# A hybrid attention block in float32 on one core: latent queries in six packed column tiles, one rope for all heads

## The chip, the cores and the metric

The kernel runs on one core of one Trainium2 chip. The metric is the device time of one execution in microseconds (us); less is better. The engines are PE (matrix multiply; PEld is its weight load), DVE (vector), ACT (scalar), POOL (GpSimd), and SP, whose queue issues nearly all DMAs here.

## The reference

One decoder layer on x of 1024 rows by 1024 columns: two parallel token mixers, gates, and a gated feed-forward block. The change touches the second mixer, multi-head latent attention (MLA), with 8 heads:

```python
cq = rmsnorm(q_lat, q_norm_g[l])                       # 1024 x 384
qb = (cq @ w_uq[l]).reshape(B, S, MLA_HEADS, MLA_QK_DIM)   # 96 = 64 + 32 per head
q_nope, q_rope = jnp.split(qb, [MLA_NOPE_DIM], axis=-1)
q_rope = apply_rope(q_rope, cos_b, sin_b)
ckv = rmsnorm(kv_lat, kv_norm_g[l])                    # 1024 x 256
kvb = (ckv @ w_ukv[l]).reshape(B, S, MLA_HEADS, MLA_NOPE_DIM + MLA_V_DIM)
k_nope, vb = jnp.split(kvb, [MLA_NOPE_DIM], axis=-1)
k_rope = apply_rope(k_r[:, :, None, :], cos_b, sin_b)[:, :, 0, :]   # one for all heads
o_b = mla_attention(q_nope, q_rope, k_nope, k_rope, vb)
```

`mla_attention` is causal softmax attention in query blocks of 128. `apply_rope` turns the two 16-wide halves x1, x2 of the 32 rope columns into x1 cos - x2 sin and x2 cos + x1 sin.

## The kernel before

Every float32 product is made of three matmuls on a high and a low part of each operand (`mm3`, lines 167 to 169), so each operand is first split: a copy on ACT (`split`, line 160) and a subtraction on DVE or POOL (line 161). The program runs in stages: input projections, sliding-window attention with the gate products woven in (`gate_step`, one product of 12 matmuls of 512 columns each), the MLA, the output projections, and the feed-forward block. In the MLA stage each engine's order of instructions is set by a scheduler at build time, from the order of the code; at run time each engine works strictly in that order, and a DMA on SP's queue waits there until its buffer or its data is ready, with all later ones behind it.

The MLA has two parts. The **front** (328 to 368 us of the trace) turns the latents round (`latent_T`, tiles lT), runs the last six gate products (tiles fa and fb; their results go are stored to memory by SP), and makes the first queries, keys and all values. Its matmul results share a pool of four PSUM buffers (`P1`) with most other tiles. Then a **loop of 64 steps**, 8 heads of 8 query blocks, follows. A step t emits the scores of step t+2 (`scores`, three matmuls for each stretch of keys), the value product of an earlier step (`pv`, tiles ob), a query or key product for a later head if one is due, and the transposes of its own probabilities (`transposes`, tiles pTb, then p split into pth and ptl). Between the scores and the transposes of a step lie a maximum on DVE (line 1148), an exponential on ACT (1149) and a division on POOL (1150, 1151).

Queries before: `prod_q(h, s)` makes, for one head h and one half s of the 1024 rows, 128 result rows in 9 matmuls of 512 columns: 64 plain rows, 32 rope rows and the same 32 with the halves swapped, from weights that hold these columns twice. One DVE product with a table (`rope_t`, tile qf) applies cosine, sine and scale; ACT and POOL split the result into qT. The scores then contract over all 128 rows, against keys whose 32 rope rows stand twice. There are 16 such tiles: two ahead of the loop, the others in steps 2 and 4 of heads 0 to 6. `prod_k(j, s)` makes the keys of two heads in 6 matmuls; each result is split for two heads, 64 rows apiece. `prod_v(b)` makes the values of one block of 128 rows for all heads in 6 matmuls; all eight stand ahead of the first scores.

## Time and profile before

| | |
|---|---|
| device time, median of three runs (range) | 1362.41 us (1362.39 to 1362.61) |
| span of the profiled execution, its own time from first to last instruction | 1359.5 us |
| PE busy | 1339.6 us, 99% of the span |
| share of PE in the chain of work that ended last | 88% |
| MLA front | 328.0 to 368.3 us |
| MLA loop, heads 0 to 6 | 368.3 to 517.9 us |

The profile is of one execution. A busy engine is not an engine at its peak: matmuls overlap, so one that is listed with 0.39 us is followed by the next after 0.23 us. A wait is named by what ended it. A window is a stretch of the span, given by its start and end; here they are the front, head 0 and heads 1 to 6 of the loop, each head from its first scores to those of the next. [...]

### The profile page before, as it was taken

What the parts mean: (1) busy time and instruction counts of PE and PEld (TensorE: products, weight loads), DVE (VectorE), ACT (ScalarE), POOL (GpSimd) and SP (SyncE); (2) the same over time, 40 slices, a digit from 0 to 9 for tenths busy, and PEclk for the clock granted to TensorE, in tenths of its full rate; (3) what the DMA queues carried; (4) which work ended last, traced back from release to release, by engine and by line L of the source; (5) the groups of instructions that cost most, each with busy time, mean ns of one, the idle gap of its engine ahead of it and who ended that gap; (6) DMA issues with size and microseconds to landing.
All of it is one profiled execution on the core that took longest, in us unless ns stands there. A gap on an engine that the chain in (4) does not pass through costs nothing.

```text
span 1359.5 us, 18989 instructions
## 1 busy us (share of the span) xinstructions
PE 1339.6 (99%) x6600; PEld 1120.0 (82%) x6600; DVE 912.7 (67%) x1495; ACT 642.8 (47%) x1299; POOL 557.7 (41%) x610
## 2 busy tenths in 40 slices
PE   9999999999999999999999999999999999999997
PEld 6899878878788888888887888888888888888886
DVE  7868767676777887585448866666656654664862
ACT  7434766675577776652336322323232332644453
POOL 2116645553166554200031465766665551022521
PEclk9999999999999999999999999999999999999999
DMA  9455322335100110671243353644434425996504
GB/s 366 154 189 163 119 86 82 113 117 182 51 2 13 44 47 17 241 239 63 105 174 132 119 181 139 235 178 169 152 144 171 170 83 183 375 382 246 170 9 147
DMA packets 78096, 202.25 MB, mean 149 GB/s; under 512 B 8753, under 2 KB 15409, under 8 KB 78001
## 3 DMA queue, kind: packets, MB, share of 16 engines
q1 hardware_dynamic: 77856, 201.04, 41.5%
q8 instruction: 52, 0.85, 0.3%
q14 instruction: 44, 0.35, 0.1%
q10 hardware_dynamic: 144, 0.00, 0.0%
HBM read 141.24 MB, written 59.77 MB: 148 GB/s over the span
## 4 chain that ended last, share of the span: by engine, by line
PE 88%; DVE 4%; issue 3%; POOL 2%; ACT 2%; DMA 0%; SPq 0%; POOLq 0%; ACTq 0%; DVEq 0%
PE fa L169 7%; PE fa L167 7%; PE fa L168 7%; PE fb L169 6%; PE fb L167 6%; PE fb L168 6%; PE fd L167 5%; PE fd L169 5%; PE fd L168 5%; PE pTb L1165 2%; PE xo L169 2%; PE xo L167 2%; PE xo L168 2%; PE ob L1188 1%; PE oA L167 1%
## 5 line engine op out<-in xcount | busy, mean ns | idle before, releaser
L161 DVE TENSOR_TENSOR wl<-wr,wl 128x512 fp32r<-128x512 f32 x150 | 153.6, 1048 | 72.2 <-ACT wl L160 71.9
L161 DVE TENSOR_TENSOR lrv<-lr,lrv 128x1024 fp32r<-128x1024 f32 x77 | 105.2, 1397 | 49.9 <-ACT lrv L160 48.8
L160 ACT CAST lrv<-lr 128x1024 fp32r<-128x1024 f32 x77 | 80.3, 1054 | 96.0 <-PE fd L169 56.0
L167 PE MATMUL fd<-lrv 128*128 128x512 f32 x308 | 119.8, 389 | 0.0
L168 PE MATMUL fd<-lrv 128*128 128x512 f32 x308 | 119.8, 389 | 0.0
L169 PE MATMUL fd<-lrv 128*128 128x512 f32 x308 | 119.8, 389 | 0.0
L172 POOL TENSOR_TENSOR wr<-wr,sm 128x512 f32<-128x512 f32 (+1 forms) x38 | 46.4, 1229 | 149.1 <-DVE wl L161 116.4
L160 ACT CAST wl<-wr 128x512 fp32r<-128x512 f32 x150 | 87.0, 624 | 2.4 <-DVE wr L820 2.2
L299 POOL TENSOR_SCALAR ms<-ss 128x1 f32<-128x1 f32 x32 | 8.8, 274 | 189.1 <-ACT xn L1534 111.7
L161 DVE TENSOR_TENSOR wl<-sm,wl 128x512 fp32r<-128x512 f32 x60 | 47.5, 818 | 45.1 <-ACT wl L160 45.0
L169 PEld LDWEIGHTS fd<-lrv 128*128 128x128 f32 x308 | 57.8, 188 | 12.1
L168 PEld LDWEIGHTS fd<-lrv 128*128 128x128 f32 x308 | 57.8, 188 | 12.1
L167 PEld LDWEIGHTS fd<-lrv 128*128 128x128 f32 x308 | 57.8, 188 | 11.8
L1150 POOL TENSOR_TENSOR denb<-denb,neg_one 128x1 f32<-128x1 f32 x64 | 36.5, 571 | 74.4 <-ACT p L1149 64.7
L1149 ACT ACTIVATE p<-scb,nmb 128x384 f32<-128x384 f32 (+3 forms) x64 | 47.6, 745 | 35.9 <-DVE nmb L1148 34.1
L161 DVE TENSOR_TENSOR ptl<-pTb,pth 128x512 fp32r<-128x512 f32 (+2 forms) x96 | 50.1, 550 | 13.8 <-ACT pth L160 13.0
L1148 DVE CUSTOM_DVE_ANT_0 scb<-scb,mask 128x384 f32<-128x384 f32 (+3 forms) x64 | 48.6, 759 | 14.0 <-PE scb L1140 13.7
L1426 ACT ACTIVATE act<-sm 128x512 f32<-128x512 f32 x11 | 7.0, 636 | 104.8 <-DVE sm L175 104.8
L1151 POOL TENSOR_SCALAR p<-p,denb 128x384 f32<-128x384 f32 (+3 forms) x64 | 49.8, 778 | 6.3
L160 ACT CAST pth<-pTb 128x512 fp32r<-128x512 f32 (+2 forms) x96 | 43.0, 483 | 13.6 <-PE pTb L1165 13.1
L167 PE MATMUL fb<-t2h,wl 128*128 128x512 f32 x120 | 47.4, 395 | 0.0
L167 PE MATMUL fb<-t3h,wl 128*128 128x512 f32 x120 | 47.3, 394 | 0.0
(346 smaller groups left out, 4287.3 us busy)
## 6 DMA issues: line engine op xcount, KB each, us to landing
lr<-la_d SPq DMA_DIRECT2D x77, 256.0 KB, 5.4
wr<-in_w_gate_dram SPq DMA_DIRECT2D x22, 512.0 KB, 3.8
wr<-in_w_up_dram SPq DMA_DIRECT2D x22, 512.0 KB, 5.0
wd<-in_w_down_dram SPq DMA_DIRECT2D x22, 512.0 KB, 6.8
rb_d<-wd SPq DMA_DIRECT2D x22, 512.0 KB, 2.6
la_d<-sd SPq DMA_DIRECT2D x22, 512.0 KB, 5.4
lr<-rb_d SPq DMA_DIRECT2D x44, 256.0 KB, 5.4
lr<-in_w_down_dram SPq DMA_DIRECT2D x33, 256.0 KB, 5.6
```

What stands on the lines that cost most here:

```text
L160: nc.scalar.copy(hi, src)
L161: (eng or nc.vector).tensor_tensor(lo, src, hi.bitcast(F32), op=ALU.subtract)
L167: nc.tensor.matmul(ps, ah, bh, start=first and i == 0, stop=False, skip_group_check=go_on)
L168: nc.tensor.matmul(ps, ah, bl, start=False, stop=False, skip_group_check=go_on)
L169: nc.tensor.matmul(ps, al, bh, start=False, stop=last and i == n - 1, skip_group_check=go_on)
L172: eng.tensor_tensor(out, a, b, op=ALU.subtract)
L1148: nc.vector.tensor_tensor_reduce(s_, s_, m_, 1.0, -NEG, op0=ALU.add, op1=ALU.min, accum_out=nm)
L1149: nc.scalar.activation(p_, s_, AF.Exp, scale=-1.0, bias=nm, accum_out=den)
L1150: nc.gpsimd.tensor_tensor(den, den, neg_one[:, 0:1], op=ALU.pow)
L1151: nc.gpsimd.tensor_scalar(p[:, 0:w], p[:, 0:w], den, 0.0, op0=ALU.mult, op1=ALU.add)
L1165: nc.tensor.transpose(pp[:, i], p[:, blk(k0 + i)], ident)
L1188: nc.tensor.matmul(po[:, q_off:], vst, lo[:, kb % 4, q_off:], start=False, stop=kb == nk - 1)
```

## The change

The query weights are packed anew in six column tiles of 128: two rope tiles (the first, and the second, 16 rope columns of all 8 heads) and four plain tiles (64 columns of two heads each). `prod_rope(s)` runs in the front: two tiles of 9 matmuls for half s, four DVE products with cosine and sine tables, a subtraction and an addition on POOL, a split on ACT and POOL, and two stores to a scratch tensor rq_d. `prod_q(j, s)` now makes two heads in 9 matmuls, splits the plain rows from PSUM for each head on ACT and DVE (`activation`, then `scalar_tensor_tensor`), and fetches each head's 32 rope rows from rq_d into rows 64 to 95 of its qT tile by two DMAs. So 12 tiles of 9 matmuls stand where 16 stood. Keys hold their rope rows once; they are split into one key tile and copied into the two others by DMA. The scores contract over 96 rows. One product `prod_q` and one `prod_k` remain ahead of the first scores, the second halves of both follow in the code, and the eight `prod_v` stand two each in steps 0 to 3. Later query products fall in step 4 of heads 0, 2, 4 and step 2 of heads 1, 3, 5. Weight units of queries are three, not four; the mask is made on POOL; loads and splits of the oa tiles stand at other steps.

```diff
+    def prod_rope(s):
+        cos, sin = (r[:, half(s)] for r in rope_cs)
+        r1, r2 = (U("rr", F32, (P, 2, 512)) for _ in range(2))
+        for i, w in enumerate(wrope):
+            ps = P1("r")
+            mm3(ps, [((w[:, 0, k], w[:, 1, k]), (cq[k][0][:, half(s)], cq[k][1][:, half(s)])) for k in range(3)])
+            nc.vector.tensor_tensor(r1[:, i], ps, sin if i else cos, op=ALU.mult)
+            nc.vector.tensor_tensor(r2[:, i], ps, cos if i else sin, op=ALU.mult)
+        sub(r1[:, 0], r1[:, 0], r1[:, 1], nc.gpsimd)
+        add(r1[:, 1], r2[:, 0], r2[:, 1], nc.gpsimd)
+        t = V("rq", F32R, (P, 2, 2, 512))
+        split(t[:, 0], t[:, 1], r1, nc.gpsimd)
+        for i in range(2):
+            nc.sync.dma_start(rq_d[i][:, :, half(s)], t[:, :, i].bitcast(F32))
...
+    for t in k_tiles:
+        if kT:
+            nc.sync.dma_start(t[64:QK].bitcast(F32), k_tiles[0][64:QK].bitcast(F32))
+        kT.append((t[:, 0], t[:, 1]))
...
+    def load_rope(h, s):
+        for i in range(2):
+            r = 64 + 16 * i
+            nc.sync.dma_start(rope_rows[h][r:r + 16, :, half(s)].bitcast(F32), rq_d[i][16 * h:16 * h + 16, :, half(s)])
+
+    def prod_q(j, s):
...
+        for h in (2 * j, 2 * j + 1):
+            load_rope(h, s)
+        w = wuq[j // 2][j % 2]
+        ps = P1("q")
+        mm3(ps, [((w[:, 0, k], w[:, 1, k]), (cq[k][0][:, half(s)], cq[k][1][:, half(s)])) for k in range(3)])
+        for u in range(2):
+            hi, lo = (t[0:64, half(s)] for t in qT[2 * j + u])
+            src = ps[64 * u:64 * u + 64]
+            nc.scalar.activation(hi, src, AF.Copy, scale=-SC_B)
+            nc.vector.scalar_tensor_tensor(lo, src, -SC_B, hi.bitcast(F32), op0=ALU.mult, op1=ALU.subtract)
...
-    def prod_q(h, s):
-        if s == 0:
-            qT[h] = hi_lo("qT")
-        w = wuq[h // 2][h % 2]
-        ps = P1("q")
-        mm3(ps, [((w[:, 0, k], w[:, 1, k]), (cq[k][0][:, half(s)], cq[k][1][:, half(s)])) for k in range(3)])
-        qf = U("qf")
-        nc.vector.tensor_tensor(qf[:, 0:512], ps, rope_t[:, half(s)], op=ALU.mult)
-        split(qT[h][0][:, half(s)], qT[h][1][:, half(s)], qf[:, 0:512], nc.gpsimd)
...
-            nc.tensor.matmul(sc[:, o], qh[:, blk(n)], kh[:, kc], start=True, stop=False)
+            nc.tensor.matmul(sc[:, o], qh[0:QK, blk(n)], kh[0:QK, kc], start=True, stop=False)
...
-    prod_k(0, 0)
-    prod_k(0, 1)
-    for b in range(NB):
-        prod_v(b)
...
+        if t < 4:
+            for b in (2 * t, 2 * t + 1):
+                prod_v(b)
...
-            if n in (2, 4):
-                prod_q(h + 1, n // 2 - 1)
+        nj = h // 2 + 1
+        if 2 * nj < NH:
+            if (h % 2, n) == (0, 4):
+                prod_q(nj, 0)
+            if (h % 2, n) == (1, 2):
+                prod_q(nj, 1)
```

PE where the first scores stand. Before (v: a value product, scb: scores):

```order
L167 MATMUL v_4155<-wv_3970,ckv_3854 128x512
L168 MATMUL v_4155<-wv_3970,ckv_3854 128x512
L169 MATMUL v_4155<-wv_3970,ckv_3854 128x512
L1138 MATMUL scb_4168<-kT_3994,qT_4037 128x384
L1139 MATMUL scb_4168<-kT_3994,qT_4037 128x384
L1140 MATMUL scb_4168<-kT_3994,qT_4037 128x384
L1138 MATMUL scb_4179<-kT_3994,qT_4037 128x512
L1139 MATMUL scb_4179<-kT_3994,qT_4037 128x512
L1140 MATMUL scb_4179<-kT_3994,qT_4037 128x512
```

And now:

```order
L168 MATMUL v_4200<-wv_4058,ckv_3936 128x512
L169 MATMUL v_4200<-wv_4058,ckv_3936 128x512
L167 MATMUL v_4210<-wv_4058,ckv_3935 128x512
L168 MATMUL v_4210<-wv_4058,ckv_3935 128x512
L1168 MATMUL scb_4135<-kT_4001,qT_4078 128x384
L1169 MATMUL scb_4135<-kT_4001,qT_4078 128x384
L1170 MATMUL scb_4135<-kT_4001,qT_4078 128x384
L1168 MATMUL scb_4164<-kT_4001,qT_4078 128x512
L1169 MATMUL scb_4164<-kT_4001,qT_4078 128x512
L1170 MATMUL scb_4164<-kT_4001,qT_4078 128x512
L169 MATMUL v_4210<-wv_4058,ckv_3935 128x512
L167 MATMUL v_4210<-wv_4058,ckv_3936 128x512
```

The first scores stand inside the second value product, where all eight stood ahead of them.

ACT in the front, ahead of the key tiles (cq and ckv: latents turned round; wl and sm: gate weights; wuq: query weights; rq: the roped rows; krT: the keys' rope rows). Before:

```order
L160 CAST wl_3919<-wr_3565 128x512
L160 CAST wl_3950<-wr_3565 128x512
L160 CAST ckv_3853<-lT_3936 128x512
L160 CAST ckv_3854<-lT_3943 128x512
L160 CAST wv_3970<-wr_3895 128x512
L160 CAST wv_3969<-wr_3895 128x512
L160 CAST wv_3970<-wr_3897 128x512
L160 CAST wv_3969<-wr_3897 128x512
L160 CAST kT_3994<-krT_3997 64x512
L160 CAST kT_3994<-krT_4008 64x512
```

And now:

```order
L160 CAST rq_3913<-rr_3885 128x1024
L160 CAST wl_3918<-sm_3676 128x512
L160 CAST ckv_3935<-lT_3937 128x512
L828 COPY go_3933<-fa_3778 128x512
L160 CAST ckv_3936<-lT_3944 128x512
L160 CAST wl_3984<-wr_3558 128x512
L160 CAST wuq_4034<-wr_3815 128x384
L160 CAST wuq_4037<-wr_3815 128x384
L160 CAST wl_4040<-wr_3558 128x512
L160 CAST rq_3979<-rr_3951 128x1024
L160 CAST kT_4001<-krT_4004 32x512
L160 CAST kT_4001<-krT_4011 32x512
```

Two casts of rq stand in the row, each of which needs POOL's sum; the second stands ahead of the casts that empty the two krT tiles.

SP's queue in the front (go: gate results, rq: rows to the scratch tensor, qT: rope rows out of it). Before:

```order
L840 DMA gate_d<-go_3891 128x512
L1058 DMA rope_t_3967<-c_rope_t_dram 128x1024
L840 DMA gate_d<-go_3891 128x512
L840 DMA gate_d<-go_3991 128x512
L1070 DMA gate_d<-go_3991 128x512
L254 DMA wr_4204<-in_w_uq_dram 128x768
```

And now:

```order
L1065 DMA rq_d<-rq_3913 256x1x512 x2
L838 DMA gate_d<-go_3933 128x512
L1065 DMA rq_d<-rq_3979 256x1x512 x2
L1084 DMA kT_4002<-kT_4001 32x2048
L1084 DMA kT_4003<-kT_4001 32x2048
L838 DMA gate_d<-go_3933 128x512
L1097 DMA qT_4078<-rq_d 16x2x512 x2
L1097 DMA qT_4079<-rq_d 16x2x512 x2
L838 DMA gate_d<-go_4075 128x512
L1122 DMA gate_d<-go_4075 128x512
L1097 DMA qT_4078<-rq_d 16x2x512 x2
L1097 DMA qT_4079<-rq_d 16x2x512 x2
```

The rope rows of the second half for heads 0 and 1 (last two rows) are issued behind the last gate store (line 1122), which stood last before too (line 1070).

## Rows read from the trace of the kernel before

**Rows 1.** page, part 1 (busy time) and part 4 (chain that ended last).
```profile
PE 1339.6 (99%) x6600; PEld 1120.0 (82%) x6600; DVE 912.7 (67%) x1495; ACT 642.8 (47%) x1299; POOL 557.7 (41%) x610
...
PE 88%; DVE 4%; issue 3%; POOL 2%; ACT 2%; DMA 0%; SPq 0%; POOLq 0%; ACTq 0%; DVEq 0%
```

**Rows 2.** windows: length, busy PE, PEld, DVE, ACT, POOL (instructions); clock, DMA, GB/s.
```profile
328.00:368.33 40.33, 40.16 (x199) 32.70 (x198) 29.61 (x48) 22.43 (x41) 2.53 (x2) 1.00 0.36 128
368.33:384.50 16.17, 15.03 (x89) 12.48 (x87) 10.92 (x25) 10.18 (x24) 10.18 (x15) 1.00 0.00 1
384.50:407.20 22.70, 22.70 (x146) 19.76 (x143) 17.71 (x38) 16.15 (x38) 14.00 (x19) 1.00 0.01 2
407.20:427.20 20.00, 19.98 (x133) 17.49 (x131) 14.66 (x32) 14.29 (x34) 12.61 (x18) 1.00 0.06 20
427.20:450.70 23.50, 22.71 (x146) 19.79 (x144) 18.47 (x38) 16.20 (x38) 13.58 (x19) 1.00 0.08 23
450.70:471.20 20.50, 20.14 (x132) 17.53 (x131) 16.67 (x34) 15.87 (x37) 11.75 (x17) 1.00 0.15 46
471.20:495.00 23.80, 22.79 (x146) 19.76 (x144) 19.69 (x42) 17.35 (x40) 14.17 (x21) 1.00 0.14 40
495.00:517.90 22.90, 21.86 (x145) 18.98 (x143) 19.97 (x38) 18.36 (x41) 12.23 (x17) 1.00 0.10 30
```

**Rows 3.** timeline of PE: start, us, instruction [idle before <- releaser].
```profile
346.67 1.04 PE L1065 MATMUL krT<-ident,lat 128*64 128x128 f32 x8
347.46 0.47 PE L167 MATMUL fa<-hh,wl 128*128 128x512 f32 x1
...
357.45 0.39 PE L167 MATMUL v<-wv,ckv 128*128 128x512 f32 x1
...
368.33 0.33 PE L1138 MATMUL scb<-kT,qT 128*128 128x384 f32 x1
...
370.50 0.50 PE L1138 MATMUL scb<-kT,qT 128*128 128x512 f32 x1 [0.78 <-ACT p L1149]
...
378.36 1.09 PE L1165 MATMUL pTb<-ident,p 128*128 128x128 f32 x8 [0.33 <-POOL p L1151]
```

**Rows 4.** timeline of PE: sliding-window scores, half of them with 64 rows.
```profile
203.80 1.23 PE L901 MATMUL sc<-khd,qs 128*128 128x256 f32 x7 [0.17 <-DVE qs L887]
204.86 0.40 PE L167 MATMUL fb<-t3h,wl 128*128 128x512 f32 x1
```

**Rows 5.** waits of PE, 340 to 545 us: total, times, longest.
```profile
PE pTb L1165 <- POOL p L1151: 1.9, 4, 0.7
PE scb L1138 <- ACT p L1149: 1.5, 2, 0.8
PE k L167 <- DVE ob L1199: 1.5, 2, 0.8
PE q L167 <- DVE ptl L161: 0.7, 2, 0.3
```

**Rows 6.** groups by tile: count, ns min/median/max, first and last start.
```profile
L1088 DVE TENSOR_TENSOR qf<-q,rope_t x16: 673/692/692, 354.0 to 518.3; 128x512 f32<-128x512 f32 x16
L161 DVE TENSOR_TENSOR kT<-k,kT x16: 677/688/694, 356.9 to 498.9; 64x512 fp32r<-64x512 f32 x16
L160 ACT CAST kT<-k x16: 567/583/586, 356.3 to 498.3; 64x512 fp32r<-64x512 f32 x16
L161 DVE TENSOR_TENSOR wl<-wr,wl x150: 674/694/1785, 128.1 to 1132.0; 128x512 fp32r<-128x512 f32 x150
L161 POOL TENSOR_TENSOR qT<-qf,qT x16: 1271/1292/1723, 355.4 to 519.7; 128x512 fp32r<-128x512 f32 x16
```

**Rows 7.** DMA issues, 300 to 560 us: KB each, us to landing.
```profile
gate_d<-go SPq DMA_DIRECT2D x9, 256.0 KB, 2.2
oa_d<-oa SPq DMA_DIRECT2D x1, 512.0 KB, 3.1
```

**Rows 8.** timeline of SP's queue: start, us, issue.
```profile
352.53 0.32 SPq L1070 DMA_DIRECT2D gate_d<-go  x1
```

More of the change, by code (lines that the diff above doesn't have):

```diff
@@ L202, in hybrid_block_kernel @@
     lat_d = dram.tile([NB, P, LAT], F32, name="lat_d")
+    rq_d = dram.tile([2, P, 2, S], F32, name="rq_d")
     gate_d = dram.tile([16, P, S], F32, name="gate_d")
@@ L287, in hybrid_block_kernel @@
         ukv_unit(k)
-    for j in range(1, 4):
-        uq_unit(j)
+    uq_unit(2)
     for nm, dp in (("oa", 0), ("oa", 1), ("oa", 2), ("ob", 0), ("ob", 1), ("oa", 3), ("ob", 2), ("ob", 3)):
@@ L1038, in latent_T @@
         split(dst[0][:, half(s)], dst[1][:, half(s)], pt.rearrange("p b c -> p (b c)"))
-    load_lat(NB)
+    rope_cs = [U("rope_cs") for _ in range(2)]
+    for t in range(2):
+        nc.sync.dma_start(rope_cs[t], c_rope_t[t])
+    wrope = st.get(("uq", 0))
+    st.load_to(st.index[("ukv", 1)])
     cq = [hi_lo("cq") for _ in range(3)]
@@ L1044, in hybrid_block_kernel @@
     gate_step()
-    ckv = [hi_lo("ckv") for _ in range(2)]
     for j in range(3):
         latent_T(j * P, cq[j], 1)
+    def prod_rope(s):
[12 more added lines that the diff above has]
+            nc.sync.dma_start(rq_d[i][:, :, half(s)], t[:, :, i].bitcast(F32))
@@ L1048, in hybrid_block_kernel @@
+    prod_rope(0)
     gate_step()
-    st.load_to(st.index[("ukv", 1)])
+    ckv = [hi_lo("ckv") for _ in range(2)]
     for j in range(2):
         latent_T(C_CKV + j * P, ckv[j], 0)
-    st.conv_to(st.index[("uq", 0)])
+    prod_rope(1)
     gate_step()
+    kT = []
+    k_tiles = [V("kT", F32R, (P, 2, S)) for _ in range(3)]
+    for s in range(2):
+        pr = P1("krT", (ROPE_B, 4, P))
+        for j in range(4):
+            nc.tensor.transpose(pr[:, j], lat[4 * s + j][:, C_RT:C_CKV], ident)
+        t = k_tiles[0][64:QK]
+        split(t[:, 0, half(s)], t[:, 1, half(s)], pr.rearrange("p b c -> p (b c)"))
@@ L1054, in hybrid_block_kernel @@
+    for t in k_tiles:
+        if kT:
+            nc.sync.dma_start(t[64:QK].bitcast(F32), k_tiles[0][64:QK].bitcast(F32))
+        kT.append((t[:, 0], t[:, 1]))
     for j in range(2):
         latent_T(C_CKV + j * P, ckv[j], 1)
+    wuq = {0: st.get(("uq", 1))}
     gate_step()
-    rope_t = U("rope_t")
-    nc.sync.dma_start(rope_t, c_rope_t)
-    st.conv_to(st.index[("ukv", 1)])
-    gate_step()
-    kT = [hi_lo("kT") for _ in range(3)]
-    for s in range(2):
-        pr = P1("krT", (HD, 4, P))
-        for j in range(4):
-            nc.tensor.transpose(pr[:, j], lat[4 * s + j][:, C_RT:C_CKV], ident)
-        for hi, lo in kT:
-            split(hi[64:128, half(s)], lo[64:128, half(s)], pr.rearrange("p b c -> p (b c)"))
+    qT = {}
@@ L1731, in _constants @@
     c, s = tables(ROPE_B)
-    rt = np.concatenate([np.ones((64, S), np.float32), c.T, c.T, -s.T, s.T]).astype(np.float32) * np.float32(-SC_B)
+    rt = np.stack([np.tile(t.T, (NH, 1)) for t in (c, s)]) * np.float32(-SC_B)
     q = np.arange(P)[:, None]
```

60 lines of the change are left out of this document (34 added, 26 removed).

## The prediction

> **What bounds the kernel now.** I read the busy times and the chain of waits first: PE is busy 99% of the span and holds 88% of the chain that ended last [rows 1]. So a matmul less is worth its price, as long as PE stays the last to be ready. Whether it does is read by stretch. In the windows PE has 40.16 of 40.33 us in the front, 15.03 of 16.17 in head 0, and in heads 1 to 6 between 20.00 and 23.80 us a head with 0.0, 0.0, 0.8, 0.4, 1.0 and 1.0 us idle [rows 2]. The reader is to see the second column there: DVE has 17.7, 14.7, 18.5, 16.7, 19.7 and 20.0 us of work in these heads, 73% to 87% of their length. PE bounds each head, with DVE some 13% behind it in head 6. The waits name what PE stops for: probabilities from POOL (1.9 us), a score buffer that ACT has to empty (1.5 us), and PSUM buffers for k and q that DVE empties late (1.5 and 0.7 us) [rows 5].
>
> **Price of a matmul.** From the first value matmul at 357.45 us to the first score at 368.33 us lie the 48 of the values: 10.88 / 48 = 0.2267 us each for 512 columns [rows 3]. Eight transposes take 347.46 - 346.67 = 0.79 us, 0.1 us each [rows 3].
>
> **The change part by part.**
>
> *Query tiles.* Before 16 x 9 = 144 matmuls, after 12 x 9 = 108: 36 x 0.2267 = 8.2 us less for PE. It is not spread evenly. Up to the end of head 0 PE now does the four rope tiles (36), three plain tiles (27), the keys (12) and the values (48): 123, where 18 + 18 + 12 + 48 = 96 stood. That is 27 x 0.2267 = **6.1 us more** there. In heads 1 to 6 twelve query tiles become five: 63 x 0.2267 = **14.3 us less**, 2.04 us in each of heads 1 to 5 and 4.08 us in head 6. So all of the gain, and the loss ahead of it, hangs on whether these six heads get shorter.
>
> *Scores over 96 rows.* No gain: seven score matmuls of 256 columns, half of them over 64 rows, take 204.86 - 203.80 = 1.06 us, 0.15 each [rows 4], which is not under the 0.11 that 256 columns cost at 0.2267 per 512. I count 0.
>
> *Values in the first steps.* Their 48 matmuls stay. Now PE idles 0.78 and 0.33 us after the first scores, waiting for ACT and POOL with nothing left to do [rows 3]; in the new order value matmuls stand between the first scores and the first transposes. I take **-1.1 us** (bounds 0 and -1.1). Their eight casts and splits go with them: two of 0.6 and 0.7 us a step on ACT and DVE, while PE gains 12 x 0.2267 = 2.7 us a step, which covers them.
>
> *The rope in the front.* It adds eight DVE products (0.69 each, by qf), on POOL four operations of 1.29 us and two of twice the columns, estimated at 2.6 us, and two ACT casts of 1024 columns, estimated at 1.2 us from 0.58 for 512 [rows 6]. It takes out two qf, four of the six key splits, and the mask on DVE. POOL has 2.53 us of work in the 40 us of the front, and DVE 29.61, so there is room [rows 2]. What can show on PE is a wait: ACT's second cast of rq waits for POOL's sums, and behind it stand the casts that empty the krT tiles, whose PSUM buffer the next gate product needs. From the last rope matmul: one DVE product 0.7, two POOL sums 2.6, the cast 1.2, the key cast 0.6, its DVE split 0.7, together 5.7 us. PE has 14 gate matmuls and 16 transposes in the meantime, 3.2 + 1.6 = 4.8 us. The rest is **+1.0 us**. Bounds: 0 (the buffer is free earlier) and 5: a weight split on DVE (wl) takes 0.694 us in the median and 1.785 at worst [rows 6], and if ten such splits of the front are each 1.1 us late because POOL is now at work, PE may wait for about half of these 11 us, DVE having 10.7 us free there. I take the 1.0, since the median wl shows nothing of it.
>
> [...]
>
> *DMAs.* New on SP's queue: four stores of 512 KB to rq_d, two key copies, 32 loads of rope rows (64 KB each). The nearest landings are 2.2 us for 256 KB and 3.1 for 512 KB [rows 7]. The last to be needed early are the second-half rope rows of heads 0 and 1, wanted by the third set of scores. They stand behind the last gate store. That was issued at 352.53 us [rows 8]; with 36 rope and 9 query matmuls now ahead of that gate product (10.2 us) and the wait of 1.0 it goes at about 363.7, four loads at 0.3 to 0.4 us behind it end at 365.3, and they land at about 368. The first scores stand at 368.33 - 0.9 (74 matmuls ahead of them, not 78) + 1.0 = 368.4, and between the first two sets and the third stand 24 value matmuls, 5.4 us: needed at about 375. Seven us of slack, so **0**.
>
> *The six heads.* PE's work falls to 20.7, 17.9, 20.7, 18.1, 20.8 and 17.8 us. DVE's hardly falls: two splits of 0.69 a tile (by kT, same rows and columns) where two qf stood [rows 6]; only in head 6 it loses a qf, 19.3 us left. POOL loses 14 x 1.29 us. If no head runs with DVE over 87% busy, the highest share now, the heads take 20.7, 17.9, 21.2, 19.2, 22.6 and 22.2 = 123.8 us against 133.4: they give back 9.6. If idle time stays as it is they give back 14.3. I take the middle, **-12.0 us**: DVE may well go past 87%, with POOL's splits gone and two of six query-weight splits left in the loop, but each query tile now holds its PSUM buffer for four operations (0.58 + 0.69, twice) instead of one of 0.69.
>
> **Sum.** +6.1 - 1.1 + 1.0 + 0 - 12.0 = -6.0 us. The profiled span of 1359.5 would become 1353.5; the median of the runs lies 2.9 us over that span, so **1356.4 us**.
>
> **Rivals.**
>
> *PE keeps the bound everywhere.* No wait in the front and heads 1 to 6 without idle: they give back 14.3, up to 14.3 + 3.2 with their present idle gone. 6.1 - 1.1 - 14.3 = -9.3, down to -12.5: 1349.9 to 1353.1 us. For it: PE is busy 95% to 100% of each head [rows 2]. Against: the waits that PE has are for DVE, ACT and POOL [rows 5], and they come nearer with less work between them. Chance 0.20.
>
> [...] Heads 1 to 6 give back 3.3 to 8.7: the time stays within 2.7 us, 0.2%, about what a measurement of this kernel can tell from no change: 1359.7 to 1365.1. For it: DVE at 87% in head 6, with 1.0 us of PE idle there already. Against: heads 1 and 2 have DVE at 78% and 73% and no idle at all. Chance 0.16.
>
> *Slower: the heads keep their pace.* If the path from scores through DVE, ACT and POOL to the transposes set the pace of a step, the 6.1 us ahead would stay and the heads would give back under 3.3: over 1365.1, up to 1362.4 + 6.0 = 1368.4. It decides where a head gives back less than a quarter of its 2.04. Against: a head with keys takes about 3 us more than one without (23.50 to 20.00), which is what its 12 matmuls cost (2.7), so PE sets the pace. Chance 0.07. Late rope rows would do the same, but need 7 + 6.0 + 2.7 = 16 us beyond the landings shown: 0.02.
>
> **How the numbers follow.** The forecast, 1353.1 to 1359.7 us, gets the rest, 0.55. It and the first rival are faster by over 0.2%: 0.75; same 0.16; slower 0.09. The range of 8 in 10 takes the forecast, most of the first rival and the lower part of the second: 1351.0 to 1361.5.
>
> **What would show it.** Right: the first scores within 1.5 us of 368.4; head 1 begins about 6 us later than now (384.5), at 389 to 391; heads 1 to 5 each 1 to 2 us shorter and head 6 some 2 us shorter, with more PE idle in head 6 than 1.0; no wait of PE on a DMA; a wait of about 1 us of a gate product after the krT transposes. Wrong: PE waiting for krT's or wl's DVE operations by several us in the front, or heads that keep 20 to 24 us with PE idle in them, or scores that wait for qT's loads.

## The result, and the profile after

The changed kernel takes 1365.95 us (median of 14 runs, 1363.69 to 1367.54), against 1362.40 for the kernel before in the same session (14 runs). The ratio is 1.0024, with a 95% interval of 1.0016 to 1.0032: slower by about 3.5 us, where 6.0 less were forecast, and above the range. The profiled spans say the same, 1359.5 before and 1363.5 after, so the steps of the prediction can be checked in one pair of traces.

The page of the changed kernel, parts 1 and 4, against [rows 1]:

```profile
PE 1336.9 (98%) x6564; PEld 1115.7 (82%) x6564; DVE 911.6 (67%) x1487; ACT 640.2 (47%) x1295; POOL 545.7 (40%) x602
...
PE 84%; DVE 4%; issue 4%; POOL 3%; ACT 2%; DMA 1%; SPq 0%; POOLq 0%; ACTq 0%; DVEq 0%
```

PE's busy time fell by only 2.7 us where 8.2 us of matmuls were taken out: a part of the rest is matmuls at a granted clock of 0.50, shown below. Its share of the chain fell by four points: waits have come in. The windows of the changed kernel show where (columns as in [rows 2]: length, busy PE, PEld, DVE, ACT, POOL, then the granted clock). The first row is the front (with 1.7 us ahead of its first transposes, which stand at 327.69 us here and at 328.00 before), then head 0, then heads 1 to 6, then two short stretches:

```profile
326.00:371.28 45.28, 42.83 (x203) 34.52 (x202) 30.77 (x46) 20.40 (x37) 12.64 (x10) 0.96 0.56 183
371.28:395.90 24.62, 22.00 (x120) 18.30 (x118) 15.60 (x31) 13.70 (x31) 8.91 (x14) 1.00 0.08 24
395.90:417.20 21.30, 20.98 (x136) 17.95 (x133) 17.55 (x38) 15.34 (x35) 8.94 (x14) 1.00 0.06 16
417.20:437.30 20.10, 18.80 (x121) 16.01 (x122) 15.77 (x33) 14.87 (x36) 11.54 (x18) 1.00 0.04 11
437.30:458.70 21.40, 20.79 (x137) 18.04 (x135) 17.50 (x38) 15.33 (x36) 9.40 (x16) 1.00 0.09 29
458.70:478.30 19.60, 18.68 (x121) 15.93 (x122) 15.56 (x33) 15.10 (x36) 11.12 (x18) 1.00 0.04 11
478.30:500.20 21.90, 21.29 (x139) 18.33 (x137) 18.19 (x39) 16.24 (x37) 9.48 (x15) 1.00 0.21 62
500.20:522.40 22.20, 18.34 (x125) 15.97 (x125) 19.91 (x41) 19.45 (x45) 10.83 (x16) 1.00 0.14 48
353.80:357.10 3.30, 3.30 (x9) 2.62 (x8) 3.04 (x6) 3.25 (x7) 2.77 (x2) 0.50 0.02 5
524.50:527.70 3.20, 3.10 (x11) 2.18 (x10) 2.29 (x6) 1.97 (x5) 2.70 (x4) 0.50 0.02 5
```

Three things are to be seen. The first scores stand at 371.3 instead of 368.3 us, and head 1 begins at 395.9 instead of 384.5: 11.4 us later, where about 6 were forecast. Heads 1 to 6 take 126.5 us instead of 133.4: 6.9 less, where 12.0 were forecast. And in two stretches the granted clock is 0.50, where it was 1.00 in each window of the MLA before [rows 2].

PE's waits between 340 and 545 us (total, times, longest), against [rows 5]:

```profile
PE pTb L1195 <- POOL p L1181: 6.5, 10, 1.4
PE scb L1168 <- ACT p L1179: 2.8, 4, 1.8
PE fb L167 <- DVE sm L175: 1.4, 1, 1.4
PE lT L1037 <- DVE rr L1059: 0.5, 1, 0.5
PE r L167 <- ACT go L828: 0.5, 1, 0.5
```

The waits for k and q of before (2.2 us) are gone; those for probabilities grew from 1.9 to 6.5 us, those for a score buffer from 1.5 to 2.8, and three in the front are new, 2.45 us together. What made the front wait is read from the timelines of DVE, POOL and ACT side by side (start, us, instruction):

```profile
344.68 2.40 DVE L161 TENSOR_TENSOR wl<-sm,wl 128x512 fp32r<-128x512 f32 x1 [3.14 <-ACT wl L160]
...
349.40 0.68 DVE L1058 TENSOR_TENSOR rr<-r,rope_cs 128x512 f32<-128x512 f32 x1
350.00 0.68 DVE L1059 TENSOR_TENSOR rr<-r,rope_cs 128x512 f32<-128x512 f32 x1
350.59 1.44 DVE L161 TENSOR_TENSOR wl<-wr,wl 128x512 fp32r<-128x512 f32 x1
351.96 0.68 DVE L175 TENSOR_TENSOR sm<-fb,pu 128x512 f32<-128x512 f32 x1
```

```profile
344.14 2.39 POOL L161 TENSOR_TENSOR rq<-rr,rq 128x1024 fp32r<-128x1024 f32 x1 [1.16 <-ACT rq L160]
350.22 1.27 POOL L172 TENSOR_TENSOR rr<-rr 128x512 f32<-128x512 f32 x1 [3.68 <-DVE rr L1058]
351.56 1.61 POOL L175 TENSOR_TENSOR rr<-rr 128x512 f32<-128x512 f32 x1
```

```profile
343.01 1.05 ACT L160 CAST rq<-rr 128x1024 fp32r<-128x1024 f32 x1 [7.68 <-POOL rr L175]
343.97 0.61 ACT L160 CAST wl<-sm 128x512 fp32r<-128x512 f32 x1
344.49 0.58 ACT L160 CAST ckv<-lT 128x512 fp32r<-128x512 f32 x1
344.96 0.59 ACT L828 COPY go<-fa 128x512 f32<-128x512 f32 x1
```

DVE's weight split at 344.68 is listed with 2.40 us where its kind takes 0.69; it ends at 347.08, half a microsecond after POOL's split (346.53). The one at 350.59 ends half a microsecond after POOL's subtraction. All that stands behind them on DVE is late: the products that free PE's rope tiles, and the gate addition sm at 351.96, for which PE then waits. But DVE was late before that. Ahead of the split at 344.68 it had stood idle for 3.14 us until ACT cast the same weights, and this cast stood on ACT behind the first cast of rq, which waited for POOL's sums. So did the copy of go, which ends the first of PE's three waits (0.51 us, at 345.60). The other two:

```profile
350.73 0.66 PE L1037 MATMUL lT<-ident,lat 128*128 128x128 f32 x4 [0.54 <-DVE rr L1059]
352.78 0.47 PE L167 MATMUL fb<-t4h,wl 128*128 128x512 f32 x1 [1.40 <-DVE sm L175]
353.09 0.40 PE L168 MATMUL fb<-t4l,wl 128*128 128x512 f32 x1
...
354.26 0.63 PE L169 MATMUL fb<-t4h,wl 128*128 128x512 f32 x1
354.69 0.63 PE L167 MATMUL fb<-t4h,wl 128*128 128x512 f32 x1
```

About a microsecond behind the second of them the granted clock falls to 0.50 (353.8 to 357.1 us). Matmuls start 0.43 us apart instead of 0.227; over the 3.3 us of the row above that loses about 3.3 x (1 - 0.227 / 0.43) = 1.6 us. At 524.5 us the same happens (0.50 to 527.7) behind waits of 1.82 and 0.74 us.

### The profile page after: what moved, and what is told of

Same layout as the page of the kernel before. It is cut to its first block, busy times and chain, and to the rows that moved or that the text cites. A ratio compares the mean times of both kernels' runs of the same rounds, so it can differ in the third digit from the quotient of the medians.

```text
span 1363.5 us, 18998 instructions
## 1 busy us (share of the span) xinstructions
PE 1336.9 (98%) x6564; PEld 1115.7 (82%) x6564; DVE 911.6 (67%) x1487; ACT 640.2 (47%) x1295; POOL 545.7 (40%) x602
## 4 chain that ended last, share of the span: by engine, by line
PE 84%; DVE 4%; issue 4%; POOL 3%; ACT 2%; DMA 1%; SPq 0%; POOLq 0%; ACTq 0%; DVEq 0%
PE fa L169 7%; PE fa L167 7%; PE fa L168 7%; PE fb L169 6%; PE fb L167 6%; PE fb L168 6%; PE fd L167 5%; PE fd L169 5%; PE fd L168 5%; PE xo L167 2%; PE xo L169 2%; PE xo L168 2%; PE pTb L1195 1%; PE oA L167 1%; PE oA L169 1%
## 5 line engine op out<-in xcount | busy, mean ns | idle before, releaser
L168 PE MATMUL fd<-lrv 128*128 128x512 f32 x308 | 119.8, 389 | 0.0
L167 PE MATMUL fd<-lrv 128*128 128x512 f32 x308 | 119.8, 389 | 0.0
L1178 DVE CUSTOM_DVE_ANT_0 scb<-scb,mask 128x384 f32<-128x384 f32 (+3 forms) x64 | 48.5, 760 | 13.6 <-PE scb L1170 12.5
L1195 PE MATMUL pTb<-ident,p 128*128 128x128 f32 x288 | 45.8, 280 | 7.2 <-POOL p L1181 6.5
L167 PE MATMUL fb<-t4h,wl 128*128 128x512 f32 x120 | 47.8, 398 | 1.4 <-DVE sm L175 1.4
```

Source lines behind the costliest of these rows:

```text
L167: nc.tensor.matmul(ps, ah, bh, start=first and i == 0, stop=False, skip_group_check=go_on)
L168: nc.tensor.matmul(ps, ah, bl, start=False, stop=False, skip_group_check=go_on)
L1178: nc.vector.tensor_tensor_reduce(s_, s_, m_, 1.0, -NEG, op0=ALU.add, op1=ALU.min, accum_out=nm)
L1195: nc.tensor.transpose(pp[:, i], p[:, blk(k0 + i)], ident)
```

## The experiments

All times of a row are from its own profile, except the median and the ratio to the kernel before (with its 95% interval), which are from the timed runs; the kernel before was timed again beside each group of runs, so the ratios are to be compared, not the medians. Where a row leaves a part of the work out, its text says so.

| kernel | median us | ratio to before | span us | first scores | head 1 begins | heads 1 to 6, us |
|---|---|---|---|---|---|---|
| before | 1362.4 | 1 | 1359.5 | 368.3 | 384.5 | 133.4 |
| changed | 1365.95 | 1.0024 (1.0016 to 1.0032) | 1363.5 | 371.3 | 395.9 | 126.5 |
| e2 rope sums on DVE | 1367.38 | 1.0033 (1.0021 to 1.0046) | 1365.6 | 371.2 | 397.4 | 127.2 |
| e8 rope sums left out | 1359.61 | 0.9974 (0.9965 to 0.9984) | 1358.1 | 364.8 | 389.2 | 126.5 |
| e10 sums on DVE, late | 1362.27 | 1.0003 (0.9994 to 1.0012) | 1359.8 | 367.5 | 392.1 | 126.6 |
| e3 values ahead | 1365.98 | 1.0028 (1.0018 to 1.0039) | 1363.5 | 380.2 | 395.9 | 126.6 |
| e4 rope rows early | 1364.54 | 1.0015 (1.0006 to 1.0024) | 1361.5 | 371.1 | 394.6 | 126.5 |
| e1 before, fewer q | 1356.33 | 0.9956 (0.9943 to 0.9968) | 1354.6 | 369.8 | 386.0 | 126.1 |
| e16 changed, fewer q | 1363.14 | 1.0004 (0.9995 to 1.0013) | 1361.7 | 371.4 | 396.1 | 124.7 |
| e14 no low part of p | 1358.68 | 0.9967 (0.9956 to 0.9979) | 1354.8 | 370.2 | 394.8 | 119.8 |
| e15 no scaling of p | 1358.90 | 0.9974 (0.9964 to 0.9984) | 1355.9 | 370.4 | 393.3 | 122.7 |
| e9 reciprocal on DVE | 1363.00 | 1.0010 (1.0001 to 1.0018) | 1362.8 | 372.0 | 396.1 | 124.9 |
| e13 same, in before | 1361.55 | 0.9992 (0.9984 to 1.0001) | 1360.2 | 369.2 | 385.1 | 132.1 |
| e5 keys spread | 1365.22 | 1.0020 (1.0011 to 1.0029) | 1362.4 | 368.2 | 393.9 | 127.4 |
| e6 splits earlier | 1364.85 | 1.0013 (1.0004 to 1.0022) | 1363.1 | 371.4 | 396.0 | 127.6 |
| e7 e4, e5, e6 joined | 1364.67 | 1.0013 (1.0004 to 1.0022) | 1362.5 | 368.0 | 394.2 | 128.7 |
| e11 e10 and e4 joined | 1361.64 | 0.9987 (0.9978 to 0.9997) | 1360.4 | 368.7 | 391.9 | 126.6 |
| e12 e11 and e9 joined | 1359.97 | 0.9984 (0.9975 to 0.9993) | 1358.2 | 367.0 | 390.2 | 124.8 |
| e17 e12 and e6 joined | 1360.76 | 0.9989 (0.9980 to 0.9998) | 1360.2 | 367.6 | 390.9 | 125.4 |

### The front: e2, e8, e10

e2 moves POOL's work in `prod_rope` to DVE. If that work is what makes DVE's weight splits long, they take 0.69 us again, and PE's three waits in the front shrink with them.

```diff
-        sub(r1[:, 0], r1[:, 0], r1[:, 1], nc.gpsimd)
-        add(r1[:, 1], r2[:, 0], r2[:, 1], nc.gpsimd)
+        sub(r1[:, 0], r1[:, 0], r1[:, 1], nc.vector)
+        add(r1[:, 1], r2[:, 0], r2[:, 1], nc.vector)
...
-        split(t[:, 0], t[:, 1], r1, nc.gpsimd)
+        split(t[:, 0], t[:, 1], r1)
```

> Changed kernel, with the two rope sums and the low split of prod_rope on DVE instead of POOL. [...] Rival, that DVE is simply overloaded or that the buffers of the rope products are what is late: DVE has some 5 us more work here, the idles stay or grow, first scores at 371 us or later.

The split of sm (344.75 in this trace) takes 0.69 us again, with POOL idle from 327.3 to 349.15 us. (The one at 350.15 takes 0.78, beside POOL's work on the mask at 349.97.) But the program is no faster, and PE's wait for the gate addition is 1.93 us, not 1.40. DVE's timeline of e2 shows what stands ahead of that addition now:

```profile
348.96 0.68 DVE L1059 TENSOR_TENSOR rr<-r,rope_cs 128x512 f32<-128x512 f32 x1
349.55 0.68 DVE L172 TENSOR_TENSOR rr<-rr 128x512 f32<-128x512 f32 x1
350.15 0.78 DVE L161 TENSOR_TENSOR wl<-wr,wl 128x512 fp32r<-128x512 f32 x1
350.85 0.68 DVE L175 TENSOR_TENSOR rr<-rr 128x512 f32<-128x512 f32 x1
351.46 0.68 DVE L175 TENSOR_TENSOR sm<-fb,pu 128x512 f32<-128x512 f32 x1
```

The durations agree with the theory that POOL's work made the split long (2.40 us beside it, 0.69 without), but moving that work this way gained nothing (1.0033 against 1.0024). e8 leaves the rope sums and the low split out (ACT casts both products, which are stored as they are), so neither POOL nor DVE has that work, to see what the long splits cost:

```diff
-        sub(r1[:, 0], r1[:, 0], r1[:, 1], nc.gpsimd)
-        add(r1[:, 1], r2[:, 0], r2[:, 1], nc.gpsimd)
...
-        split(t[:, 0], t[:, 1], r1, nc.gpsimd)
+        nc.scalar.copy(t[:, 0], r1)
+        nc.scalar.copy(t[:, 1], r2)
```

> Changed kernel whose rope sums and low split are left out (the products are cast by ACT and stored as they are), so that POOL does nothing in the front; DVE keeps all its work there, ACT gets two casts of 1024 columns more. [...] Rival, that the order of DVE's queue (rope products ahead of the gate add) is what is late: the wait of 1.40 us stays over 0.8 us with every split at 0.69, and the first scores stand at 370 us or later.

The weight splits wl of the front take 0.69 us, PE's three waits and the first fall of the clock are gone (1.00 from 340 to 365 us), sm stands at 348.05, and the first scores at 364.8. That is 6.5 us ahead of the changed kernel, but the build-time order changed as well: ten key and value matmuls (2.3 us) now stand behind the first scores. Where head 1 begins this falls out: 6.7 us earlier, of which 2.3 are waits in the front, 2.3 waits in head 0 and 1.6 the clock. By the ratios, POOL's part of the rope and what hung on it cost 0.50%, some 6.8 us. e8 does not tell the long splits from the place of the work in the queues; e10, set against e2, does. It has the sums and splits on DVE as e2 has, but writes them later:

```diff
+        return r1, r2
+
+    def rope_end(s, r1, r2):
...
+    rope0 = prod_rope(0)
     gate_step()
...
     gate_step()
+    rope_end(0, *rope0)
...
     gate_step()
+    rope_end(1, *rope1)
     qT = {}
```

> Changed kernel with the rope sums and low splits on DVE, as in the earlier run, but written one gate product (first half) and two transposes and a gate product (second half) later, behind the gate additions that PE waited for. If the order in DVE's queue is what made PE wait in that run (1.93 us for a gate addition), first scores stand at 365 to 368 us instead of 371.2 and the time falls to 1361 to 1363.5 us (ratio 0.999 to 1.0005). If DVE's work in the front is too much in sum (5.2 us more), first scores stay at 370 to 372 us and the time at 1365 to 1367 us.

DVE's timeline of e10, at the same place as that of e2 above; ACT's, where the cast of rq stood first in the changed kernel; and the one wait of PE that is left in the front:

```profile
348.10 0.68 DVE L1059 TENSOR_TENSOR rr<-r,rope_cs 128x512 f32<-128x512 f32 x1
349.19 0.69 DVE L161 TENSOR_TENSOR wl<-wr,wl 128x512 fp32r<-128x512 f32 x1 [0.41 <-ACT wl L160]
349.80 0.68 DVE L175 TENSOR_TENSOR sm<-fb,pu 128x512 f32<-128x512 f32 x1
```

```profile
342.55 0.59 ACT L160 CAST ckv<-lT 128x512 fp32r<-128x512 f32 x1 [0.78 <-PE lT L1037]
343.27 0.62 ACT L160 CAST wl<-sm 128x512 fp32r<-128x512 f32 x1
343.80 1.05 ACT L160 CAST rq<-rr 128x1024 fp32r<-128x1024 f32 x1
344.85 0.59 ACT L828 COPY go<-fa 128x512 f32<-128x512 f32 x1
```

```profile
PE fb L167 <- DVE sm L175: 0.4, 1, 0.4
```

The same work on the same engine, written later, moves the first scores from 371.2 to 367.5 us, and the time from 1.0033 to 1.0003 of before. (Some 1.6 of the 3.7 us are the clock: from 340 to 365 us its mean is 0.93 in e2 and 1.00 in e10.) DVE is not too full in the front: it is the order that counts, and in the changed kernel the splits of 2.40 and 1.44 us worked like a bad order, by holding back what stood behind them, sm among it. The edit moved two things at once, the sums on DVE from ahead of sm and the cast of rq on ACT from ahead of the weights and latents; no run moved one alone, so how the gain divides between them is not shown.

### Head 0: e3 and e4

e3 puts the eight `prod_v` and the second query and key tiles ahead of the first scores again.

> Changed kernel, with the eight value products, the second query tile and the second key tile ahead of the first scores again, as before. Head 0 was 8.5 us longer with the values in it, while the values' matmuls are 10.9 us and the two tiles 4.8. If the place of the values costs nothing beyond their matmuls (the prediction had it as 1.1 us of gain), the time rises by about 1 us (1367 us, ratio 1.0033). If the waits of 1.36 and 1.19 us in head 0 come from that place (first transposes and third scores queued around them), the time falls by 1 to 2.5 us (1363.5 to 1365 us).

```diff
+    prod_q(0, 1)
+    prod_k(0, 1)
+    for b in range(NB):
+        prod_v(b)
     psum_phase("psb", 2)
     scores(0)
-    prod_q(0, 1)
     scores(1)
-    prod_k(0, 1)
```

Head 1 begins at the same 395.9 us, and the ratios cannot be told apart. PE's waits between the first scores and head 1 are 2.55 us in the changed kernel (1.36 and 1.19, both for p from POOL); in e3 two of 0.8 and 1.2 us are the longest. So the move fills the waits of before with values and leaves others of the same size. It is neither the gain that the prediction took nor the loss that I expected here. (In e3 the front has the same waits, 0.49, 0.54 and 1.40 us, but the clock stays at 1.00; its first rope matmul starts 0.8 us later, and both count in the 395.9.)

e4 loads the rope rows of both halves with the first.

```diff
-        for h in (2 * j, 2 * j + 1):
-            load_rope(h, s)
+        for i in ((0, 1) if s == 0 else ()):
+            for h in (2 * j, 2 * j + 1):
+                load_rope(h, i)
```

> Changed kernel, with the rope rows of both halves of a pair of heads loaded where the first half's were, so the second half's go ahead of the last gate store on SP's queue. If these rows decide where the third scores may stand, the third scores come earlier than 380.4 us, the wait of 1.19 us in head 0 goes and the time falls by about 1 us (ratio about 1.0015). If they have slack, as the prediction took it, nothing changes (1365.5 to 1366.5 us, ratio 1.002 to 1.003), or SP's queue delays the first half's rows instead and PE waits for them ahead of the first scores.

The third scores stand at 378.6 instead of 380.4, the wait of 1.19 us is gone, and head 0 takes 23.4 instead of 24.6 us. The time falls by 0.0009 of the ratio, with intervals that overlap; the trace is what shows it. PE never waited for these rows in either kernel. The order that the scheduler wrote down placed the third scores behind 24 value matmuls and two groups of transposes; with the loads ahead of the last gate stores it placed them earlier.

### Heads 1 to 6: how much PE counts (e1, e16)

e1 cuts the query tiles of heads 2 to 7 in the kernel before from 9 matmuls to 4, e16 the last five tiles in the changed kernel; both leave most of the contraction out.

```diff
...
+            mm3(ps, [((w[:, 0, 0], w[:, 1, 0]), (cq[0][0][:, half(s)], cq[0][1][:, half(s)]))], last=False)
+            nc.tensor.matmul(ps, w[:, 0, 1], cq[1][0][:, half(s)], start=False, stop=True)
```

> Kernel before, with the query tiles of heads 2 to 7 cut from 9 matmuls to 4 (most of the contraction left out; nothing else moves): 12 tiles x 5 x 0.2267 = 13.6 us less for PE in heads 1 to 6. If PE alone bounds these heads, as the -12.0 of the prediction took it, the six heads become about 13 us shorter and the time falls to about 1349 us (ratio 0.990). If the path from scores through DVE, ACT and POOL to the transposes is close behind PE, the heads give back about half, 6 to 8 us (1354.5 to 1356.5 us, ratio 0.995 to 0.996), and PE's idle time on p and on the score buffers grows by the rest.

> Changed kernel with the last five query tiles, those of heads 1 to 5, cut from 9 matmuls to 4 (most of the contraction left out): 25 x 0.2267 = 5.7 us less for PE. If PE still sets these heads, they give back 5 to 5.7 us (ratio 0.998 to 0.9985). If what is beside PE sets them by now, they give back 0 to 2.5 us (ratio 1.0005 to 1.0024), less per matmul than the same cut in the kernel before (5.9 of 13.6).

The window of head 1 and the sum over heads 1 to 6, in e1 (columns as above):

```profile
386.00:407.80 21.80, 21.00 (x135) 17.74 (x133) 18.10 (x38) 16.11 (x38) 14.11 (x19) 1.00 0.01 2
...
sum 126.10, PE 120.33 PEld 101.85 DVE 106.35 ACT 97.85 POOL 77.84; mean PE 20.06 PEld 16.98 DVE 17.72 ACT 16.31 POOL 12.97
```

e1: heads 1 to 6 fall by 7.3 us of 13.6 (54%), the time, by the ratio, by 6.0 (44%); over the whole profile e1 has a mean granted clock of 0.997 and the kernel before one of 0.998, with 1.00 in each of heads 1 to 6 in both. Head 1, where PE had no idle time at all, gives back 0.9 us of 2.3. So already in the kernel before, whose heads PE kept busy for 95% to 100%, a matmul less was worth about half its price. e16: heads 1 to 5, where the cut tiles stand, give back 2.5 us of 5.7 (44%). Head 6 takes 0.7 us longer, with a granted clock of 0.93 in its window. The price per matmul is thus about half in both kernels, and no smaller price after the change is to be seen. The change's own 6.9 of 14.3 us is 48%.

### Heads 1 to 6: what stands beside PE (e14, e15, e9, e13)

e14 leaves out the low part of the transposed probabilities: DVE's split goes, and the value product multiplies the high part twice, so PE's work stays. e15 leaves out POOL's inverse and scaling of p.

```diff
-            split(hi[:, 0:m, blk(odd)], lo[:, 0:m, blk(odd)], pp[:, 0:m])
+            nc.scalar.copy(hi[:, 0:m, blk(odd)], pp[:, 0:m])
...
-            nc.tensor.matmul(po[:, q_off:], vst, lo[:, kb % 4, q_off:], start=False, stop=kb == nk - 1)
+            nc.tensor.matmul(po[:, q_off:], vst, hi[:, kb % 4, q_off:], start=False, stop=kb == nk - 1)
```

```diff
-        nc.gpsimd.tensor_tensor(den, den, neg_one[:, 0:1], op=ALU.pow)
-        nc.gpsimd.tensor_scalar(p[:, 0:w], p[:, 0:w], den, 0.0, op0=ALU.mult, op1=ALU.add)
```

> Changed kernel without the low split of the transposed probabilities on DVE (the value product multiplies the high part twice; PE's work stays): some 5.4 us of DVE's 17.5 us a head fall away, and each step's scores are taken up sooner. If DVE's queue sets the length of heads 1 to 6, PE's waits there nearly vanish and they take 118 to 121 us instead of 126.5 (about 1358 to 1360 us, ratio 0.997 to 0.9985). If ACT and POOL do, they get at most 2 us shorter (1364 us, ratio 1.001 or more).

> Changed kernel without POOL's part of a step (the inverse and the scaling of p are left out; the transposes take p from ACT): each step's path from scores to transposes is 0.9 to 1.7 us shorter. If the length of this path sets the heads, PE's waits nearly vanish and heads 1 to 6 take 118 to 121 us (ratio 0.997 to 0.9985). If it is work in DVE's or ACT's queue, they get at most 2 us shorter (ratio 1.001 or more), as the reciprocal's 1.7 us already hints.

The windows of heads 1 and 2 and the sum over heads 1 to 6, first of e14, then of e15 (columns as above):

```profile
394.80:415.20 20.40, 20.38 (x135) 17.99 (x134) 12.25 (x26) 15.45 (x36) 10.24 (x16) 1.00 0.05 14
415.20:434.30 19.10, 17.84 (x123) 15.96 (x122) 9.78 (x21) 14.73 (x35) 10.38 (x17) 1.00 0.05 15
...
sum 119.80, PE 114.87 PEld 102.17 DVE 72.63 ACT 95.43 POOL 60.72; mean PE 19.14 PEld 17.03 DVE 12.11 ACT 15.90 POOL 10.12
```

```profile
393.30:414.60 21.30, 20.78 (x135) 18.06 (x133) 17.52 (x38) 15.34 (x35) 0.00 (x0) 1.00 0.06 17
414.60:433.90 19.30, 18.75 (x121) 15.99 (x122) 15.10 (x33) 14.82 (x36) 0.00 (x0) 1.00 0.04 11
...
sum 122.70, PE 117.94 PEld 102.45 DVE 102.96 ACT 95.85 POOL 0.00; mean PE 19.66 PEld 17.07 DVE 17.16 ACT 15.98 POOL 0.00
```

Without the DVE splits the six heads take 119.8 us, 6.7 less, in the band expected if DVE's queue sets them; head 1 has PE busy for 20.38 of 20.40 us. Without POOL's part they take 122.7, 3.8 less: between the two expectations. So both lie on the path, DVE with more, and neither of my pure theories holds. PE's idle time in head 2 (1.3 us) stays at 1.3 in e14, where it waits for p from POOL, and falls to 0.6 in e15. The same matmuls are listed with 118.9 us of PE in the changed kernel and with 114.9 in e14, so some 4 us of what the windows count as busy there were not PE's own work.

e9 takes the inverse on DVE, a reciprocal of 128x1 instead of POOL's 0.56 us; e13 does it in the kernel before.

```diff
-        nc.gpsimd.tensor_tensor(den, den, neg_one[:, 0:1], op=ALU.pow)
+        nc.vector.reciprocal(den, den)
```

> Changed kernel with the inverse of the softmax sum taken by DVE (a reciprocal of 128x1) instead of by POOL (0.56 us each, 56 times); POOL still scales p by it. If the path from scores through DVE, ACT and POOL to the transposes is what PE waits for in the heads, each step's path is some 0.4 us shorter, PE's waits for p (3.9 us from head 1 on) fall to half or less, and heads 1 to 6 take 2 to 4 us less than 126.5 in sum: 1362 to 1364 us (ratio 1.0 to 1.001). If DVE's work in sum sets their length, 56 more operations of 0.1 to 0.15 us on DVE make them up to 6 us longer (1366 us or above, ratio 1.0025 or more).

> Kernel before with the same reciprocal on DVE and nothing of the change. There PE waited for p for only 1.9 us in heads 0 to 7, so the shorter path can give back 1 us at most: 1361.5 to 1363 us (ratio 0.9992 to 1.0003). If it gains as much here as in the changed kernel, the path sets the pace of the heads with or without the change, which would speak against the theory that the change uncovered it.

Heads 1 to 6 get 1.6 us shorter in the changed kernel and 1.3 in the one before. PE's waits for p hardly fall (3.9 to 3.5 us from head 1 to 525 us), against what I expected. And the gain is about the same with and without the change, which speaks against my theory that the change had uncovered this path: it was there before.

### Edits that moved waits only (e5, e6, e7)

> Changed kernel with a fourth buffer of keys, so that of each pair's two key tiles the first stands in the even head before (0, 2, 4) instead of with the second in the odd head. PE's work and DVE's stay the same in sum. Theory, that a head gives back too little because too little work of PE without a wait stands between a step's scores and its transposes: in the even heads the key tile of 1.4 us lies in the waits for p (about 1.3 us in head 2, 1.0 in head 4), the odd heads get 0.7 to 1.4 us shorter each, heads 0 to 6 together 1.5 to 3 us shorter, about 1363 to 1364.5 us (ratio 1.0005 to 1.0015). Rival, that the work of DVE and ACT in a head sets its length wherever PE's tiles stand: the even heads get longer by what the odd ones lose, and the time stays at 1366 us (ratio 1.0025 to 1.003).

> Changed kernel with the splits of the attention output (wv and obT) taken out of heads 6 and 7 into heads 4 to 6, nothing added. If their cluster on ACT and DVE is what PE waits for at the end of head 6 (1.82 and 0.74 us, and the clock at half speed behind them), head 6 takes 20 to 21 us instead of 22.2, PE's waits there fall under 0.5 us and the time falls by 1.5 to 3.5 us (1362.5 to 1364.5 us, ratio 1.0 to 1.0015). If all heads are bound by DVE's and ACT's work in sum, heads 4 and 5 get longer by what head 6 loses and nothing is gained.

> Changed kernel with the fourth buffer of keys, the earlier splits and the rope rows of both halves loaded early, all three together. If their gains lie in different heads they add: 1.4 us from the rows (measured), 1.5 to 3 from the keys, 1.5 to 3.5 from the splits, so 4.5 to 8 us below the changed kernel, 1358 to 1361.5 us, faster than the kernel before (ratio 0.997 to 0.9995). If one path sets the pace of all heads, the gains overlap and it stays at 1362 us or above (ratio 1.0 or more).

```diff
...
-            if n in (3, 5) and h % 2 == 1:
-                prod_k(nj, n // 2 - 1)
+            if (h % 2, n) == (0, 6):
+                prod_k(nj, 0)
+            if (h % 2, n) == (1, 5):
+                prod_k(nj, 1)
```

```diff
...
-        if -3 <= e < 3:
-            split_ob((e + 3) // 2, (e + 3) % 2)
+        if e in OB_SPLIT:
+            split_ob(*OB_SPLIT[e])
```

e5 tells little: the scheduler put the key tile that was written into the even head behind the first value products of the odd head, so the even heads never held it. In e6 head 6 takes 22.4 us and head 5 22.7 (21.9 before the edit); only the stretch behind head 6 got shorter. But in these two profiles of e6 and e7 the stretch at the lower clock lies inside head 6 (granted clock 0.92 in its window), where it costs about 1.6 us, while in the changed kernel it lies behind it (0.50 from 524.5 us, 1.00 in head 6); so head 6 of e6 is not known to the microsecond. e7 does not add the three up: heads 1 to 6 take 128.7 us, and the time is that of e4 alone.

### Joined versions (e11, e12, e17)

> Changed kernel with three edits together: the late rope sums on DVE, the rope rows of both halves loaded early, the reciprocal on DVE. They act in the front, in head 0 and in heads 1 to 6; if each works as its theory says they add up to 5 to 9 us below the changed kernel, 1357 to 1361 us, under the kernel before (ratio 0.996 to 0.999). If the front's DVE work or the heads' DVE work is the bound, it stays at 1363 us or above (ratio 1.0005 or more).

> The three edits of e12 (late rope sums on DVE, early rope rows, reciprocal on DVE) with the earlier splits of the attention output added. If the splits' gain of the earlier run (1.1 us of ratio) adds, 1358 to 1359.5 us (ratio 0.997 to 0.998); if they only move the same work among full heads, as when three edits were joined before, about 1360 us (ratio 0.9984).

> Changed kernel with the late rope sums on DVE and the rope rows of both halves loaded early, without the reciprocal. If the front's and head 0's edits add (ratio 1.0003 for the first, 0.0009 for the second), about 0.9994, 1361.5 us: level with the kernel before, so that the gain of the joined version (0.9984) is the reciprocal's. If it is 0.9988 or below, the mended change is faster by itself.

These are made of the diffs above. e12 is the fastest that leaves nothing out: 0.9984 of before, about 2.2 us less. e11, without the reciprocal, is at 0.9987 (0.9978 to 0.9997): with its front and its rope rows mended the change is a gain, if one of under 0.3%. The earlier splits of e17 add nothing.

## Why the prediction was wrong, step by step

- **6.1 us more up to the end of head 0: right.** With the rope's sums out of the way (e8) head 1 begins at 389.2 us, inside the 389 to 391 of the prediction. Without PE's waits, front and head 0 take 61.2 us there and 55.2 before, 6.0 more. The count of matmuls and their price held.
- **The rope in the front, +1.0: wrong, the first of two steps that failed.** It took 2.45 us of waits and 1.6 us at a granted clock of 0.50. The prediction had one path right, from POOL's sums over ACT's cast of rq to what stands behind it; but it looked at the second cast and the krT tiles. It was the first cast that held back the latents, the weights and the copy of go. The gate product behind the krT transposes did wait, 1.40 us, but for sm on DVE, whose queue was late from there on and was held up twice at its weight splits. The bound of 5 had such long splits, beside POOL at work, and was set aside because "the median wl shows nothing of it". The median was read rightly, but it was the wrong figure: the page of the kernel before lists the same 150 splits with a mean of 1048 ns:

```profile
L161 DVE TENSOR_TENSOR wl<-wr,wl 128x512 fp32r<-128x512 f32 x150 | 153.6, 1048 | 72.2 <-ACT wl L160 71.9
```

In the trace of before 68 of them took over 0.8 us, each beside an instruction of POOL; a median of 150 hides 68. In the front the same was seen: 2.40 us beside POOL's work in the changed kernel, 0.69 us in e2 with POOL idle. But e10 shows that the damage came through what stood behind, on DVE and on ACT. For the loop, where the -12.0 counted with POOL's splits gone, no run tells what they were worth.
- **Values in the first steps, -1.1: wrong.** Two waits of 0.78 and 0.33 us [rows 3] went, and two of 1.36 and 1.19 came, 2.6 us off the forecast. e3 shows that the values' place is worth nothing that these runs can tell; e4 shows that one of the two new waits hung on where the rope rows were loaded.
- **Rope rows, 0 with seven microseconds of slack: right for the wait, incomplete as a cost.** No wait on a DMA appeared. But the build-time order counted with these loads, and that kept the third scores back by 1.8 us, as e4 shows.
- **Scores over 96 rows, 0: right.** In the changed trace such matmuls of 512 columns start at 517.43, 517.67 and 517.90 us, 0.23 to 0.24 apart.
- **Heads 1 to 6, -12.0: wrong, the second step, and the larger.** They gave back 6.9, under the lower bound of 9.6: PE's busy time fell by 11.3 us (130.2 to 118.9), and its idle time grew by 4.4 (3.2 to 7.6). By the head the bound had 20.7, 17.9, 21.2, 19.2, 22.6 and 22.2 us, and they took 21.3, 20.1, 21.4, 19.6, 21.9 and 22.2: most of what is missing is head 2, which got no shorter at all. The bound assumed that PE sets the length until DVE is over 87% busy. By the windows DVE is at 78% to 83% in heads 1 to 5 (78% in head 2), yet PE is idle there. A busy share under 87% does not say that DVE is never the last in a step. e1 shows the same half price in the kernel before, e14 and e15 that DVE's and POOL's parts of a step are worth 6.7 and 3.8 us beside PE. The rival with the chance of 0.16 had the right size for the heads (3.3 to 8.7), but also a wrong test, "no idle at all" in heads 1 and 2: PE could be busy throughout and still not be what a matmul less would shorten (in head 1 of e1, 0.9 us of 2.3). That each query tile holds its PSUM buffer for longer did not show: the waits for k and q (2.2 us before) went.
- **The rivals.** The time lies in the band of "slower: the heads keep their pace" (chance 0.07), but not for its reason: that wanted heads that give back under 3.3 us, and they gave back 6.9; by the head, only heads 2 and 6 gave back less than a quarter of what their matmuls cost. Another had heads that give back 3.3 to 8.7, and the bounds of the front went up to 5; the front's 4.05 us and the heads' 6.9 came together, with 2.6 in head 0 besides, and no rival counted with the sum.
- **The clock: not in the prediction.** Two stretches at 0.50, some 1.6 us each in the profiled execution.

The sum in the profile: 5.4 us too late at head 1, of which 1.5 more wait in the front than the 1.0, 1.6 the clock and 2.6 head 0 (5.7; the front also begins 0.3 earlier), and 5.1 too little from heads 1 to 6; behind them 0.5 was gained. -6.0 + 5.4 + 5.1 - 0.5 = +4.0, the difference of the spans.

**What stays open.** Why the clock fell here and not in e3, behind the same waits; it need not be the edit, since executions of one kernel differ (see the last section). How the front's loss divides between the long splits on DVE and the cast on ACT. Why head 2 gave back nothing. And which part of a step would have to go first for PE's full price to be paid: e14 and e15 take single parts out, and no run took both.
